# Attention scores on two row halves, and TensorE's order in periods of three pairs

## The chip, the cores and the metric

The kernel runs on one core of a Trainium2 chip. A core has TensorE (matmuls; PE in the profile, its weight loads PEld), VectorE (DVE), ScalarE (ACT), GpSimd (POOL) and SyncE (SP, which here issues the DMAs). Each engine works through its own queue in order and waits on semaphores for the others. TensorE writes to PSUM, eight banks of 128 partitions x 512 numbers of 32 bits. The metric is the time of one execution in microseconds (us), as the median of several runs; a profiled execution is recorded beside them.

## The reference

One layer of a hybrid backbone over 2048 latent tokens of width 1024 and 256 context tokens: a modulated norm, one input projection, two groups of heads, one output projection, and a SwiGLU FFN. The group that is changed is a softmax attention of 8 query heads on 2 key heads (4 query heads each), head width 64, over 2304 keys (context and latent):

```
def block(q):
    s = jnp.einsum('bqkgd,bnkd->bkgqn', q, keys).astype(jnp.float32) * scale
    p = jax.nn.softmax(s, axis=-1)
    return jnp.einsum('bkgqn,bnkd->bqkgd', p.astype(vals.dtype), vals)

o = lax.map(block, qb)
```

The other group is a gated linear recurrence in both directions over the same tokens (4 heads of width 128); its output and the attention's are concatenated ahead of the output projection.

## The kernel before, in words

An **item** is one query tile (128 queries) of one key head with its 4 query heads: 16 tiles x 2 key heads = 32 items. Keys come in 18 tiles of 128. Queries and keys are split in a high and a low part, since one pass of a matmul of the type used (fp32r) rounds its operands.

The softmax needs the maximum ahead of the exponentials, so an item passes over the scores twice.

*First pass* (`Item.chunk`, nine calls per item, one item ahead). A chunk takes 512 keys and two heads: two matmuls on 64 rows each (high part of the queries against high part of the keys), the one on rows 0 to 63, the other on rows 64 to 127 of the array, into two PSUM banks of one tile `mx` (line 930; the pool has one buffer). VectorE reduces the tile to `mn` (lines 936 and 940). The ninth chunk takes the last 256 keys for all four heads. `maxima` transposes the result (`pn`), copies it (`mr`) and writes it by four small DMAs into row 0 of `qb`.

*Second pass* (`Item.scores`, once for each key tile). Two matmuls on all 128 rows: `KS` (high and low key parts on the two halves) against `qa` (the high queries on both), line 962, and `KB` (a row of -1 and the high keys) against `qb` (the maximum and the low queries), line 963. ScalarE takes the Exp of the tile `s` (three banks) into half of a pair tile `p` (line 965). `KB` holds the high keys of one key head at a time and is loaded again where the second begins, and items 16 and 17 therefore compute their maximum on all 128 rows of `KS`. GpSimd adds two pair tiles of three (`ps`, line 972). `products` multiplies six key tiles with the values (line 981) and sums the weights by columns of ones (line 989) into one bank `av`; `finish` spreads the reciprocals (`pb`, line 1002) and scales the output.

*The order around it.* TensorE's order is the order of the program's text in this stage (a manual schedule); the other engines' order is set by the framework's scheduler. A tick is one key tile of one item. At each tick stand the scores, then steps of the recurrence (six of every nine ticks), then whatever `events` holds for the tick: chunks at ticks -3, -1, 0, 2, 3, 5, 7, 9 and 11 of the item before, loads and `maxima`. Every sixth tick has `products`, every ninth a round of the recurrence (`pa`, line 646), which reaches all engines. The recurrence shares two PSUM banks (`ps_h`) with `pn` and `pb`.

## Time and profile before

| what | value |
|---|---|
| median of 3 runs | 3408.22 us (3406.96 to 3409.92) |
| profiled execution | 3398.26 us |
| its span, first to last instruction | 3396.5 us |
| mean granted TensorE clock | 0.982 |
| attention stage, first scores to last | about 756 to 1842 us of the span |
| TensorE busy, whole span | 3235.6 us |
| first pass' reductions on VectorE (L936) | 256 of 1223 ns |
| Exp on ScalarE (L965) | 576 of 596 ns |

Rows of TensorE in the profile give the start, the duration, the line, the operation with what it writes and reads, the part of the array (rows*columns), the shape, and the count of instructions merged. Matmuls overlap with the next, so the distance of two starts is what one costs. `[0.18 <-DVE mn L936]` is idle time just before, and what ended it. A row of windows gives the stretch, the busy us of the five engine columns, the granted clock, the DMA share and GB/s. A row of groups gives busy us and the mean in ns after the first bar, idle us before it after the second.

### The profile page before, as it was taken

The numbers are of one execution on the slowest core, as the hardware profiler recorded it, in microseconds if no ns is written. First come the engines' busy times: TensorE is split into PE (matmuls) and PEld (weight loads), VectorE is DVE, ScalarE is ACT, GpSimd is POOL, SyncE is SP. The second block draws the span as 40 slices with busy tenths as digits, with TensorE's granted clock in tenths as the row PEclk, the third lists the DMA queues.
The fourth block names the chain that finished last, engine by engine and source line by source line (L and its number), as shares of the span: only waits on it lengthen the run. The fifth ranks groups of instructions, "written<-read, shape, count | busy, mean of one in ns | idle before, by whom it ended". The sixth has DMA issues, their size and how long they took to land. (4 is left out here: it accounts for less than half of the span.)

```text
span 3396.5 us, 55490 instructions
## 1 busy us (share of the span) xinstructions
PE 3235.6 (95%) x21212; PEld 2514.5 (74%) x21212; DVE 1725.5 (51%) x2742; ACT 1303.6 (38%) x2559; POOL 1636.5 (48%) x1450
## 2 busy tenths in 40 slices
PE   7999999979999999999999999999989989999998
PEld 5998977965666666656667887788868768888887
DVE  6344555224555455555553557444465743333566
ACT  4322222214444444444443224333344443333444
POOL 4322223105666666666644218776631357666222
PEclk9999999989999999999999999999989999999999
DMA  7243445341111111201105444444475543323754
GB/s 238 86 150 125 136 143 150 94 135 35 29 34 43 52 39 42 63 28 46 31 16 157 132 142 131 154 152 158 159 253 188 187 128 103 100 95 103 255 197 161
DMA packets 364459, 396.75 MB, mean 117 GB/s; under 512 B 30848, under 2 KB 261216, under 8 KB 363808
## 3 DMA queue, kind: packets, MB, share of 16 engines
q1 hardware_dynamic: 364192, 393.20, 36.2%
q8 instruction: 166, 2.72, 0.3%
q14 instruction: 101, 0.83, 0.1%
HBM read 271.90 MB, written 121.13 MB: 116 GB/s over the span
## 5 line engine op out<-in xcount | busy, mean ns | idle before, releaser
L936 DVE TENSOR_REDUCE mn<-mx 128x2 f32<-128x1024 f32 x256 | 313.2, 1223 | 418.8 <-PE mx L930 322.3
L965 ACT ACTIVATE p<-s 128x512 f32<-128x512 f32 x576 | 326.8, 596 | 469.8 <-PE s L963 467.9
L972 POOL TENSOR_TENSOR ps<-p,p 128x1024 f32<-128x1024 f32 x96 | 228.4, 2379 | 276.7 <-ACT p L965 276.5
L962 PE MATMUL s<-qa,K 128*128 128x512 f32 x576 | 271.3, 471 | 0.0
L981 PE MATMUL av<-p,VS 128*64 128x256 f32 x2304 | 270.6, 384 | 0.0
L963 PE MATMUL s<-qb,KB 128*128 128x512 f32 x576 | 232.5, 404 | 4.0 <-DMA KB<-s_k 3.2
L981 PEld LDWEIGHTS av<-p,VS 128*64 128x64 f32 x2304 | 158.1, 138 | 86.8 <-issue 15.7
L1500 POOL TENSOR_TENSOR y<-y,yg 128x512 f32<-128x512 f32 x48 | 76.1, 1600 | 284.1 <-DVE yg L1499 280.3
L930 PE MATMUL mx<-K,qa 64*128 64x512 f32 (+3 forms) x340 | 151.5, 470 | 63.3 <-DVE mn L936 63.2
L930 PEld LDWEIGHTS mx<-K,qa 64*128 64x128 f32 (+1 forms) x340 | 61.1, 190 | 163.9 <-DVE mn L936 127.7
L962 PEld LDWEIGHTS s<-qa,K 128*128 128x128 f32 x576 | 109.9, 191 | 71.1 <-issue 41.5
L1469 DVE TENSOR_TENSOR x<-lr,x 128x512 fp32r<-128x512 f32 x154 | 119.8, 813 | 67.2 <-ACT x L1468 64.5
L1469 DVE TENSOR_TENSOR dl<-lr,dh 128x512 fp32r<-128x512 f32 x154 | 118.6, 809 | 64.9 <-ACT dh L1468 64.8
L930 PE MATMUL mx<-KB,qa 64*128 64x512 f32 x300 | 138.9, 479 | 0.0
L1468 ACT ACTIVATE dh<-lr 128x512 fp32r<-128x512 f32 x154 | 89.4, 623 | 109.0 <-PE pd1A L1523 51.8
L343 PE MATMUL f<-hTh,wh 128*128 128x512 f32 (+1 forms) x320 | 122.4, 382 | 7.4 <-ACT ft L372 7.4
L1468 ACT ACTIVATE x<-lr 128x512 fp32r<-128x512 f32 x154 | 90.5, 626 | 93.8 <-PE pd0A L1523 38.5
L1330 PE MATMUL pA<-x,A11h 128*128 128x512 f32 x352 | 113.7, 403 | 9.7 <-ACT A11h L1303 7.4
L963 PEld LDWEIGHTS s<-qb,KB 128*128 128x128 f32 x576 | 111.2, 193 | 13.6 <-DMA KB<-s_k 3.5
L1523 PE MATMUL pd0A<-x,x 128*128 128x512 f32 x528 | 120.7, 389 | 0.0
L343 PE MATMUL f<-hTh,wl 128*128 128x512 f32 (+1 forms) x320 | 119.8, 375 | 0.0
L343 PE MATMUL f<-hTl,wh 128*128 128x512 f32 (+1 forms) x320 | 119.7, 374 | 0.0
(345 smaller groups left out, 9238.1 us busy)
## 6 DMA issues: line engine op xcount, KB each, us to landing
w<-in_w_gu_dram SPq DMA_DIRECT2D x88, 512.0 KB
wm<-in_w_mod_dram SPq DMA_DIRECT2D x24, 1024.0 KB
lr<-s_wT SPq DMA_DIRECT2D x88, 256.0 KB
lr<-in_w_down_dram SPq DMA_DIRECT2D x66, 256.0 KB
wq<-in_w_down_dram SPq DMA_DIRECT2D x44, 256.0 KB
s_wT<-wq SPq DMA_DIRECT2D x44, 256.0 KB
lr<-s_hid1S SPq DMA_DIRECT2D x44, 256.0 KB
lr<-s_hid0S SPq DMA_DIRECT2D x44, 256.0 KB
```

Source lines behind the costliest of these rows:

```text
L343: nc.tensor.matmul(pm[:, :n], w[wi][:, k, c0:c0 + P], hT[b][hi][:, k, :], start=(k == 0 and i == 0), stop=(k == KT - 1 and i == 2))
L930: nc.tensor.matmul(s[:, i, o:o + n], self.qa[ps, (h0 + i) * P:(h0 + i + 1) * P], K[ps, k0:k0 + n], start=True, stop=True)
L936: nc.vector.tensor_reduce(self.mn[:, h:h + 2, k], s, axis=AX.X, op=ALU.min)
L962: nc.tensor.matmul(s, KS[self.g][:, ks], self.qa, start=True, stop=False)
L963: nc.tensor.matmul(s, KB[:, ks], self.qb, start=False, stop=True)
L965: nc.scalar.activation(self.pairs[p][:, o:o + 512], s, AF.Exp, scale=-1.0)
L972: nc.gpsimd.tensor_tensor(t, self.pairs[p - 1], self.pairs[p], op=ALU.add)
L981: nc.tensor.matmul(self.av[i * 64:(i + 1) * 64, :256], VS[:, k, self.g * 64:(self.g + 1) * 64], self.pairs[k // 2][:, o:o + 256], start=(k ...
L1330: nc.tensor.matmul(acc, w[wi][:, k, :], x[xi][k], start=(start and k == 0 and i == 0), stop=(stop and k == KH - 1 and i == 2), skip_group_ ...
L1468: nc.scalar.activation(hi, src, AF.Copy)
L1469: nc.vector.tensor_tensor(lo, src, f32v(hi), op=ALU.subtract)
L1523: nc.tensor.matmul(cur[t], l[:, t * P:(t + 1) * P], r, start=(start and j == 0 and f == 0), stop=(stop and j == NHF - 1 and f == 2), skip_ ...
```

## The change

Second pass: a call of `scores` now makes a pair of key tiles, the even one on rows 0 to 63 and the odd one on rows 64 to 127. Four steps (high keys with high queries, low keys with high queries, high keys with low queries, and a row of -1 with the maximum) are each two matmuls on 64 rows, into two PSUM banks; the pool still has three. Keys are stored with the even tiles ahead of the odd ones; `KH` and `KL` hold the parts of both key heads for the whole stage, `KM` the row of -1, and `QM` the maximum, which is written once for each half (eight DMAs). Low queries are loaded on both halves.

First pass: a chunk is one head and 384 columns of both halves, so there are twelve per item, reduced in one go to one number.

Order: a period is three pairs and the products of these pairs; it has four chunks, one per quarter, and four steps of the recurrence. The first pair of the next period stands ahead of the products. The Exp's, sums and products themselves stay.

```
 def load_low(self):
-                self.qb = QB[self.n % 2]
-                nc.sync.dma_start(f32v(self.qb[64:, :]), s_q[self.g][self.qt, 1].rearrange("d h x -> d (h x)"))
+                self.qb = qpl.tile([P, 512], F32R, tag="qb", name=f"qb{self.nm}", bufs=2)
+                self.twice(self.qb, 1)
...
-                if c < 8:
-                    h, k = c // 4 * 2, c % 4
-                    part(0, h, k * 512, 512)
-                    nc.vector.tensor_reduce(self.mn[:, h:h + 2, k], s, axis=AX.X, op=ALU.min)
...
+                h, k = divmod(c, 3)
+                for i in range(2):
+                    rw = slice(i * 64, (i + 1) * 64)
+                    nc.tensor.matmul(s[:, i, :384], self.qa[rw, h * P:(h + 1) * P],
+                                     KH[self.g][rw, k * 384:(k + 1) * 384], start=True, stop=True)
+                nc.vector.tensor_reduce(self.mn[:, h, k:k + 1], s[:, :, :384], axis=AX.XY, op=ALU.min)
...
-                nc.tensor.matmul(s, KS[self.g][:, ks], self.qa, start=True, stop=False)
-                nc.tensor.matmul(s, KB[:, ks], self.qb, start=False, stop=True)
...
+                s = [ps_st.tile([P, 512], F32, tag="s", name=f"s{self.nm}_{p}{i}") for i in range(2)]
+                hi, lo = (K[self.g][:, p * P:(p + 1) * P] for K in (KH, KL))
+                ops = (hi, self.qa), (lo, self.qa), (hi, self.qb), (KM, self.qm)
+                for f, (k, q) in enumerate(ops):
+                    for i in range(2):
+                        rw = slice(i * 64, (i + 1) * 64)
+                        nc.tensor.matmul(s[i], k[rw, :], q[rw, :], start=(f == 0), stop=(f == 3))
+                for i in range(2):
+                    nc.scalar.activation(t[:, i * 512:(i + 1) * 512], s[i], AF.Exp, scale=-1.0)
...
-        CHUNKS = (-3, -1, 0, 2, 3, 5, 7, 9, 11)
...
+        chunks = {12 * (n - 1) - 5 + c: (it, c) for n, it in enumerate(items) if n for c in range(12)}
...
+                chunk(4 * x)
+                if b == 0 and n:
+                    items[n - 1].drain()
+                item.scores(GP * b + 1)
+                rest(0)
+                chunk(4 * x + 1)
+                rest(1)
+                item.scores(GP * b + 2)
+                if b == 0 and n:
+                    items[n - 1].finish(ps_h, "h")
+                chunk(4 * x + 2)
+                rest(2)
+                if x + 1 < NPER * NIT:
+                    items[(x + 1) // NPER].scores((x + 1) % NPER * GP)
+                made = rest(3)
+                if b == 1 and n + 1 < NIT:
+                    items[n + 1].maxima()
+                chunk(4 * x + 3)
+                next(made, 0)
+                item.products(b)
+                next(made, 0)
```

`rest(i)` makes one step of the recurrence, or a round of it at every sixth; `drain` copies the finished output and takes the reciprocals.

TensorE in item 12, just behind the products of item 11, before. A name `s12_0_3` is query tile 12, key head 0, key tile 3; `mx13_0_4` is chunk 4 of the next item.

```order
L962 MATMUL s12_0_3_12123<-qa12_0_11569,K0_7774 128x512
L963 MATMUL s12_0_3_12123<-qb0_7778,KB_7776 128x512
L930 MATMUL mx13_0_4_12129<-K0_7774,qa13_0_11945 128x512
L930 MATMUL mx13_0_4_12129<-KB_7776,qa13_0_11945 128x512
L962 MATMUL s12_0_4_12134<-qa12_0_11569,K0_7774 128x512
L963 MATMUL s12_0_4_12134<-qb0_7778,KB_7776 128x512
L962 MATMUL s12_0_5_12139<-qa12_0_11569,K0_7774 128x512
L963 MATMUL s12_0_5_12139<-qb0_7778,KB_7776 128x512
L930 MATMUL mx13_0_5_12143<-K0_7774,qa13_0_11945 128x512
L930 MATMUL mx13_0_5_12143<-KB_7776,qa13_0_11945 128x512
```

The same place now, where `s12_0_10` and `s12_0_11` are the two halves of pair 1:

```order
L930 MATMUL mx13_0_5_12772<-Kh0_7774,qa13_0_12329 128x384 x2
L957 MATMUL s12_0_10_12781<-qa12_0_11882,Kh0_7774 128x512
L957 MATMUL s12_0_11_12782<-qa12_0_11882,Kh0_7774 128x512
L957 MATMUL s12_0_10_12781<-qa12_0_11882,Kl0_7776 128x512
L957 MATMUL s12_0_11_12782<-qa12_0_11882,Kl0_7776 128x512
L957 MATMUL s12_0_10_12781<-qb12_0_12332,Kh0_7774 128x512
L957 MATMUL s12_0_11_12782<-qb12_0_12332,Kh0_7774 128x512
L957 MATMUL s12_0_10_12781<-qm0_7780,KM_7778 128x512
L957 MATMUL s12_0_11_12782<-qm0_7780,KM_7778 128x512
L930 MATMUL mx13_0_6_12799<-Kh0_7774,qa13_0_12329 128x384 x2
L957 MATMUL s12_0_20_12804<-qa12_0_11882,Kh0_7774 128x512
L957 MATMUL s12_0_21_12805<-qa12_0_11882,Kh0_7774 128x512
```

Chunks and scores are now alike in rows and columns of the array; between two pairs stands one chunk.

ScalarE at the same place before:

```order
L965 ACTIVATE p12_0_1_12082<-s12_0_2_12083 128x512
L965 ACTIVATE p12_0_1_12082<-s12_0_3_12123 128x512
L996 ACTIVATE ot11_0_12121<-av11_0_11856 128x256
L965 ACTIVATE p12_0_2_12133<-s12_0_4_12134 128x512
L965 ACTIVATE p12_0_2_12133<-s12_0_5_12139 128x512
```

And now, with the recurrence's M and C ahead of pair 1:

```order
L959 ACTIVATE p12_0_0_12682<-s12_0_00_12683 128x512
L959 ACTIVATE p12_0_0_12682<-s12_0_01_12684 128x512
L672 ACTIVATE M13_3_12913<-C13_2_12746 128x32x8
L619 ACTIVATE C14_0_12981<-F14_12795 128x512
L672 ACTIVATE M12_7_12924<-C12_6_12757 128x2x128
L673 ACTIVATE C13_4_13145<-C13_3_12914 128x16x2x8
L991 ACTIVATE ot11_0_12776<-av11_0_12459 128x256
L959 ACTIVATE p12_0_1_12780<-s12_0_10_12781 128x512
L959 ACTIVATE p12_0_1_12780<-s12_0_11_12782 128x512
```

The two Exp's of a pair follow each other, and work for the recurrence stands between pairs.

TensorE ahead of the first scores, before:

```order
L948 MATMUL pn0_0_7843<-identr_107,neg0_0_7841 4x128
L930 MATMUL mx1_0_0_7855<-K0_7774,qa1_0_7851 128x512
L930 MATMUL mx1_0_0_7855<-KB_7776,qa1_0_7851 128x512
L930 MATMUL mx1_0_1_7859<-K0_7774,qa1_0_7851 128x512
L930 MATMUL mx1_0_1_7859<-KB_7776,qa1_0_7851 128x512
L962 MATMUL s0_0_0_7868<-qa0_0_7794,K0_7774 128x512
```

And now:

```order
L941 MATMUL pn0_0_7866<-identr_107,neg0_0_7864 4x128
L930 MATMUL mx1_0_0_7879<-Kh0_7774,qa1_0_7808 128x384 x2
L930 MATMUL mx1_0_1_7883<-Kh0_7774,qa1_0_7808 128x384 x2
L930 MATMUL mx1_0_2_7887<-Kh0_7774,qa1_0_7808 128x384 x2
L930 MATMUL mx1_0_3_7891<-Kh0_7774,qa1_0_7808 128x384 x2
L930 MATMUL mx1_0_4_7895<-Kh0_7774,qa1_0_7808 128x384 x2
L957 MATMUL s0_0_00_7900<-qa0_0_7797,Kh0_7774 128x512
```

Five chunks of item 1 stand ahead of the first pair instead of two.

## The prediction

> **What bounds the kernel now.** I read the page first, then windows over the program's stages, then TensorE's own rows inside the stage that the change touches, then who waited for whom there.

> ```profile
> PE 3235.6 (95%) x21212; PEld 2514.5 (74%) x21212; DVE 1725.5 (51%) x2742; ACT 1303.6 (38%) x2559; POOL 1636.5 (48%) x1450
> 727.00:756.00 29.00, 8.44 (x29) 3.38 (x27) 16.41 (x20) 3.92 (x7) 5.62 (x5) 0.59 0.53 138
> 756.00:1842.00 1086.00, 1025.67 (x10009) 676.82 (x10010) 568.56 (x794) 494.42 (x1038) 667.89 (x711) 0.98 0.15 43
> ```

> TensorE is the bound of the whole program (95%) and of the attention stage, which lasts from 756 to 1842 us: 1026 of 1086 us there, while VectorE has 569, ScalarE 494 and GpSimd 668. Ahead of it lie 29 us of prelude in which TensorE works 8. All that changes lies in these 1115 us. A busy TensorE is not one at its peak, so I read starts, not durations:

> ```profile
> 1210.13 0.40 PE L963 MATMUL s<-qb,KB 128*128 128x512 f32 x1
> 1210.45 0.49 PE L930 MATMUL mx<-K,qa 64*128 64x512 f32 x1
> 1210.46 0.49 PE L930 MATMUL mx<-KB,qa 64*128 64x512 f32 x1
> 1210.88 0.50 PE L962 MATMUL s<-qa,K 128*128 128x512 f32 x1
> 1211.22 0.40 PE L963 MATMUL s<-qb,KB 128*128 128x512 f32 x1
> 1211.46 0.40 PE L962 MATMUL s<-qa,K 128*128 128x512 f32 x1
> 1211.69 0.40 PE L963 MATMUL s<-qb,KB 128*128 128x512 f32 x1
> 1212.28 0.39 PE L930 MATMUL mx<-K,qa 64*128 64x256 f32 x1 [0.18 <-DVE mn L936]
> 1212.28 0.50 PE L930 MATMUL mx<-KB,qa 64*128 64x256 f32 x2
> 1212.50 0.27 PE L930 MATMUL mx<-K,qa 64*128 64x256 f32 x1
> 1212.71 0.50 PE L962 MATMUL s<-qa,K 128*128 128x512 f32 x1
> ```

> Inside a run of scores, matmul follows matmul by 0.23 us (1211.46 to 1211.69). Around a maximum's chunk, which uses half the rows (64*128 beside 128*128), the steps are 0.32 (1210.13 to 1210.45), 0.42 and 0.34: 1.08 us instead of 3 x 0.23 = 0.69. So one chunk between scores costs 0.39 us for two changes of the array's setting, 0.20 each. The two halves of a chunk start 0.01 us apart, so they do run together.

> **Removed: changes of setting.** Counted along TensorE's order of this stage, 851 changes become 665: between full and half height 497 become 317, the others 354 become 348. 180 x 0.20 = **-36 us**. The scores' own work is the same: a pair of key tiles was 4 matmuls on full height and is now 8 on half height, two at a time: 4 steps of 0.23 both ways. The maximum streams the same 4608 columns per item and half (8 x 512 + 2 x 256 before, 12 x 384 after).

> **Removed: full-height chunks and one load.** Two items (16 and 17) computed their maximum on full height, one half after the other:

> ```profile
> L930 PE MATMUL mx<-K,qa 128*128 128x512 f32 x32 | 11.4, 439 | 4.0 <-DVE mn L936 4.0
> L930 PE MATMUL mx<-K,qa 128*128 128x256 f32 x8 | 1.4, 294 | 1.3 <-DVE mn L936 1.3
> ```

> They now take half the steps: 16 x 0.23 + 4 x 0.12, **-4 us**. The second head group's keys now have buffers of their own, so the single 3.2 us wait for KB goes (row below): **-3 us**.

> **Added: scores in pairs on three PSUM banks.** A pair takes two banks; with three in rotation, the second half's first matmul of the next pair needs the bank that the first Exp of this pair frees. TensorE goes in order, so everything behind stands still too.

> ```profile
> 1210.56 0.60 ACT L965 ACTIVATE p<-s 128x512 f32<-128x512 f32 x1 [2.96 <-PE s L963]
> 1211.66 1.09 ACT L965 ACTIVATE p<-s 128x512 f32<-128x512 f32 x2 [0.50 <-PE s L963]
> 1210.99 1.23 DVE L936 TENSOR_REDUCE mn<-mx 128x2 f32<-128x1024 f32 x1 [3.32 <-PE mx L930]
> 1212.27 0.18 PEld L930 LDWEIGHTS mx<-K,qa 64*128 64x128 f32 x1 [0.62 <-DVE mn L936]
> ```

> From the start of a pair's last matmul: 0.40 until it ends (1210.13 to 1210.53), 0.03 to the Exp, 0.60 for it, 0.05 back to TensorE (the reduction ends at 1212.22, the weight load that waits for it starts at 1212.27): 1.08 us, plus 0.11 for a weight load that waited and so isn't hidden. Without a wait the next pair would start 0.23 + 0.17 (a chunk of 384 columns) later. So 1.19 - 0.40 = 0.79 us are lost where only a chunk stands between two pairs. In the changed order 192 places have no products between two pairs; 74 of them hold nothing but a chunk (20 between pairs 1 and 2 of an item, 11 between 7 and 8, 1 between 4 and 5, 16 between 5 and 6, 26 between 8 and the next item's 0). The other 118 hold work of the recurrence or of the normaliser (L1002, the row is below) as well: 0.47 us for this one, or 0.2 in the smallest, with two changes of setting of 0.20 each, and that covers the wait. After a pair that itself began staggered (11 of the 26), the first half ends one step earlier: 0.55. 63 x 0.79 + 11 x 0.55 = **+56 us**. The ends: 0 if ScalarE were ahead, which its 0.60 excludes, and 192 x 0.79 = 152 if nothing covered. I keep 56, since the count is of places and the price of rows.

> ```profile
> 1202.41 0.71 PE L1002 MATMUL pb<-li,pick 128*128 128x128 f32 x4
> 1202.88 0.48 PE L962 MATMUL s<-qa,K 128*128 128x512 f32 x1
> ```

> **Moved: the maximum's chunks.** They were bunched, the waits for them are these:

> ```profile
> PE mx L930 <- DVE mn L936: 44.2, 95, 3.6
> PE s L963 <- DMA KB<-s_k: 3.2, 1, 3.2
> PE pn L948 <- DVE o L769: 3.1, 3, 1.2
> PE pn L948 <- DVE neg L943: 2.7, 1, 2.7
> PE pn L948 <- DVE Sb L739: 1.1, 1, 1.1
> ```

> Most of the 95 are of the 0.2 us kind seen at 1212.28; that part, some 14 us, lies inside the bare gaps from now on and is not paid twice: **-14**. The rest, 30 us, are a few long ones of this kind:

> ```profile
> 1020.23 0.95 DVE L994 RECIPROCAL li<-av 128x128 f32<-128x128 f32 x1
> 1021.09 0.11 DVE L683 TENSOR_REDUCE T<-T 128x8 f32<-128x16 f32 x1
> 1021.70 1.22 DVE L683 TENSOR_REDUCE T<-F 128x512 f32<-128x1024 f32 x1 [0.49 <-DMA F<-s_f]
> 1022.83 0.34 DVE L711 SCALAR_TENSOR_TENSOR S<-S,T,psf 128x128 f32<-128x128 f32 x1
> 1023.09 1.22 DVE L936 TENSOR_REDUCE mn<-mx 128x2 f32<-128x1024 f32 x1
> ```

> Here the recurrence's new unit stands ahead of the maximum in VectorE's queue and itself waits for its load. The changed order has the same operations in that queue, with 12 reductions per item instead of 9. I leave the 30 us where they are. The reductions shrink from 1024 to 768 elements (1.22 to about 0.92, an estimate by elements) and rise in number, 11.0 us per item both ways. New short waits: the last chunk of a period where neither a bare gap nor other work precedes it (12 places) and the transpose of the maximum (8 places), 0.4 each, 8 us, against the 7 us of pn that they replace: **+2** with rounding up.

> **Added: ScalarE's queue counts.** Before, a score tile could be two tiles ahead of ScalarE; now each pair leans on the Exp just before it, so an operation of the recurrence ahead of an Exp is felt at once.

> ```profile
> L672 ACT ACTIVATE C<-C 128x256 f32<-128x256 f32 x111 | 47.1, 424 | 20.6 <-POOL C L668 8.9 <-POOL kk L625 8.1
> L618 ACT ACTIVATE C<-F 128x512 f32<-128x512 f32 x15 | 10.2, 683 | 0.4
> ```

> One such 0.4 to 0.7 us in half of 32 items is **+8 us**; between 0 and the 30 us of a second set of long waits.

> **Prelude.** VectorE sets its pace, with TensorE's clock down (0.59 in the window):

> ```profile
> 749.05 1.23 DVE L936 TENSOR_REDUCE mn<-mx 128x2 f32<-128x1024 f32 x1 [0.89 <-PE mx L930]
> 751.17 1.23 DVE L940 TENSOR_REDUCE mn<-mx 128x4 f32<-128x1024 f32 x1 [0.89 <-PE mx L930]
> 753.83 1.23 DVE L936 TENSOR_REDUCE mn<-mx 128x2 f32<-128x1024 f32 x1 [1.22 <-PE mx L930]
> ```

> A chunk takes 2.12 us; one of 384 columns about 1.7. Twelve instead of nine: 20.4 against 19.1. Then five chunks of item 1 instead of two stand ahead of the first scores: 8.5 against 4.3, of which 1.6 is work that is missing later. **+5 us**, with bounds 0 and 8. Eight row copies of the maximum instead of four, and the low queries loaded twice, go through SyncE while five chunks or a whole period pass; with DMA at 0.15 of its time in the stage they cost nothing, and if that cover were gone, the one late copy per item would stop an item's first pair.

> **Sum.** -36 - 4 - 3 + 56 - 14 + 2 + 8 + 5 = **+14 us**. The profiled execution took 3398.3 us (span 3396.5), so 3412 for the like of it; the median of the runs shown lies 10 us higher, at 3408.2, so **3422 us**. A measurement of this kernel tells about 0.2% (7 us) from no change.

> One price has no row: the step of accumulating pairs on half height. The nearest is the second half-height step above: 1212.28 to 1212.50, 0.22 with 0.11 of unhidden load and 256 columns, so 0.11 for 256 and about 0.22 for 512 instead of 0.23; that would give up to 1152 x 0.01 = 11 us. I take 0.23 and keep the 11 for the range.

> **Rivals.**

> *Faster (0.31).* Spreading dissolves the long waits: a chunk now has a pair (0.93 us) or more before its bank is needed again, and the products (3.7 us) stand behind the fourth. If the 30 us go and the step is 0.22: 3422 - 30 - 11 = 3381; with half of that, about 3400. For it: 95 waits came from chunks one or two key tiles apart. Against: the long ones reach 3.6 us, more than a pair covers. It decides when more than 21 of the 30 us go.

> *No change (0.11).* A third of that, or bare gaps of 0.6 instead of 0.79: 74 x 0.19 = 14 us, 3408.

> *Much slower by queues (0.12).* Each of the 16 units' starts stops ScalarE or VectorE once more for 2 us, now also for the pairs: +32, 3454.

> *Weight loads come into the open (0.05).* If a half could not load its next weights while it streams, each of 1152 steps would grow by the 0.11 us that a visible load costs (0.34 against 0.23): 3422 + 127 = 3549. Against it:

> ```profile
> 1212.38 0.19 PEld L930 LDWEIGHTS mx<-K,qa 64*128 64x128 f32 x1
> 1212.39 0.19 PEld L930 LDWEIGHTS mx<-KB,qa 64*128 64x128 f32 x1
> ```

> Both halves' second weights load from 1212.38 while the first weights, loaded from 1212.28, stream on the same rows, and the next matmul starts at 1212.50. [...]

> **How the numbers follow.** Likeliest is the sum (0.41 with its own range 3408 to 3445). With the two slower rivals, slower by over 0.2% gets 0.58, no change 0.11, faster 0.31. The range from 3376 to 3470 leaves out the open weight loads and the tails.

> **What would show it.** Right: half-height scores 0.23 us apart, a new line of TensorE waiting for ScalarE's Exp of 50 us or more, waits for the maximum still above 30 us, the first scores about 5 us later. Wrong: waits for the maximum under 15 us (then faster), or steps of 0.34 between pairs' matmuls (then much slower).

## The result and the profile after

The changed kernel takes **3432.66 us** (median of 6 runs, 3424.65 to 3437.35), the kernel before beside it 3407.59 (6 runs, 3392.04 to 3411.95). The ratio is **1.0093 (95% interval 1.0071 to 1.0115)**: slower by 0.9%, some 32 us (24 to 39). The two medians as they stand lie 25 us apart. The forecast was 3422.

Profiled execution of the changed kernel, the page's first line and two windows, the prelude and the attention stage:

```profile
PE 3255.6 (95%) x22492; PEld 2551.3 (75%) x22492; DVE 1743.8 (51%) x2838; ACT 1298.3 (38%) x2559; POOL 1635.9 (48%) x1451
727.00:760.00 33.00, 11.81 (x52) 6.27 (x50) 16.26 (x23) 4.18 (x8) 5.65 (x5) 0.62 0.48 126
760.00:1870.00 1110.00, 1041.85 (x11279) 711.03 (x11280) 590.75 (x888) 490.79 (x1039) 673.72 (x712) 0.97 0.16 46
```

TensorE stays the bound, with 20 us more of busy time, and its clock in the stage is 0.97 where it was 0.98. The span grew by 27.5 us, from 3396.5 to 3424.0. Where, by the starts of single instructions:

| stretch | before | after | difference |
|---|---|---|---|
| span's start to first chunk of a maximum | 727.2 | 729.6 | +2.4 |
| prelude: first chunk to first scores | 28.6 | 35.3 | +6.7 |
| first scores to last products | 1091.2 | 1113.3 | +22.1 |
| last products to first matmul of the FFN (`pA`) | 189.0 | 184.6 | -4.4 |
| from there to the end | 1360.5 | 1361.2 | +0.7 |

Some 3 of the +22.1 us are work that only moved: 32 matmuls of the output projection now stand ahead of the last products where it was 19 (13 of 0.23 us), and the stretch behind is shorter for it.

The place where two pairs have only a chunk between them, TensorE's rows of the changed kernel and ScalarE's row beside it:

```profile
956.03 0.50 PE L957 MATMUL s<-qa,Kh 64*128 64x512 f32 x2
956.36 0.40 PE L957 MATMUL s<-qa,Kl 64*128 64x512 f32 x2
956.60 0.40 PE L957 MATMUL s<-qb,Kh 64*128 64x512 f32 x2
956.83 0.40 PE L957 MATMUL s<-qm,KM 64*128 64x512 f32 x2
957.07 0.33 PE L930 MATMUL mx<-Kh,qa 64*128 64x384 f32 x2
957.24 0.39 PE L957 MATMUL s<-qa,Kh 64*128 64x512 f32 x1
957.91 0.49 PE L957 MATMUL s<-qa,Kh 64*128 64x512 f32 x1 [0.28 <-ACT p L959]
957.91 0.72 PE L957 MATMUL s<-qa,Kl 64*128 64x512 f32 x2
958.25 0.62 PE L957 MATMUL s<-qb,Kh 64*128 64x512 f32 x2
958.49 0.62 PE L957 MATMUL s<-qm,KM 64*128 64x512 f32 x2
957.26 1.09 ACT L959 ACTIVATE p<-s 128x512 f32<-128x512 f32 x2 [0.53 <-PE s L957]
```

The first pair runs both halves together, 0.23 us from step to step (956.36, 956.60, 956.83). The chunk follows with no change of the array's setting, 0.24 after them. The first half of the next pair starts at 957.24 in the bank that was free; the second waits until the first Exp (957.26, two of 0.6 in the row) has emptied its bank, and starts at 957.91. From then on the halves are a step apart: the row at 958.49 covers 0.62 us with two matmuls of 0.39, so the last starts at 958.72. From a pair's last matmul (956.83) to the next pair's last it is 1.88, which is also the median over the 76 such places that the trace shows (11 of them take 1.65 to 1.76); without a wait it would be 1.10 (0.17 for the chunk, 0.93 for the pair).

Waits of TensorE between the first scores and the last products (matmuls), and of its weight loads; the last line is that of the kernel before:

```profile
PE mx L930 <- DVE mn L932: 31.8, 19, 4.9
PE s L957 <- ACT p L959: 9.1, 30, 0.5
PE mt L1136 <- DMA mix<-s_hg: 6.2, 3, 2.5
PEld mx L930 <- DVE mn L932: 81.7, 106, 5.3
PEld s L957 <- ACT p L959: 36.5, 85, 0.9
PEld s L962 <- ACT p L965: 11.8, 43, 0.4
```

The 95 waits for a maximum (44.2 us) became 19 (31.8 us, of which 1.05 still ahead of the first scores). Those under 1 us fell from 22 us to 4; those over 1 us were 12 with 22 us and are 12 with 27 us in the stage. The weight loads waited for the Exp before as well, 11.8 us, and do so for 36.5 now. New is a wait of 6.2 us for `mix`, the input of the output projection, near the stage's end. The longest wait for a maximum, on TensorE and then on VectorE, with the clock behind it:

```profile
854.91 0.39 PE L957 MATMUL s<-qm,KM 64*128 64x512 f32 x2
860.22 0.69 PE L930 MATMUL mx<-Kh,qa 64*128 64x384 f32 x2 [4.92 <-DVE mn L932]
858.08 1.22 DVE L684 TENSOR_REDUCE T<-F 128x512 f32<-128x1024 f32 x1 [4.77 <-DMA F<-s_f]
859.22 0.95 DVE L932 TENSOR_REDUCE mn<-mx 128x1 f32<-128x768 f32 x1
860.00:865.00 5.00, 4.78 (x46) 3.43 (x48) 3.55 (x7) 1.14 (x3) 4.99 (x8) 0.52 0.02 3
865.00:870.00 5.00, 4.87 (x63) 3.16 (x61) 2.11 (x3) 1.77 (x4) 3.13 (x6) 1.00 0.00 2
```

VectorE's queue has the recurrence's unit (`T<-F`) ahead of the maximum's reduction. `F` has one buffer, its load lands 4.77 us after VectorE could have begun, and TensorE, whose next chunk needs the tile `mx`, stands for 4.92 us. Then it runs at half clock (0.52) for the next window of 5 us, and at full clock after that.

### The profile page after: what moved, and what is told of

It is laid out like the page before. It is cut to its first block, busy times and chain, and to the rows that moved or that the text cites. A ratio compares the mean times of both kernels' runs of the same rounds, so it can differ in the third digit from the quotient of the medians.

```text
span 3424.0 us, 58458 instructions
## 1 busy us (share of the span) xinstructions
PE 3255.6 (95%) x22492; PEld 2551.3 (75%) x22492; DVE 1743.8 (51%) x2838; ACT 1298.3 (38%) x2559; POOL 1635.9 (48%) x1451
## 5 line engine op out<-in xcount | busy, mean ns | idle before, releaser
L932 DVE TENSOR_REDUCE mn<-mx 128x1 f32<-128x768 f32 x384 | 366.4, 954 | 441.1 <-PE mx L930 440.4
L959 ACT ACTIVATE p<-s 128x512 f32<-128x512 f32 x576 | 312.8, 594 | 442.4 <-PE s L957 437.0
L930 PE MATMUL mx<-Kh,qa 64*128 64x384 f32 x768 | 173.2, 431 | 62.9 <-DVE mn L932 53.7
L930 PEld LDWEIGHTS mx<-Kh,qa 64*128 64x128 f32 x768 | 77.8, 190 | 144.6 <-DVE mn L932 110.3
L957 PE MATMUL s<-qa,Kh 64*128 64x512 f32 x576 | 163.4, 453 | 9.7 <-ACT p L959 9.1
L957 PE MATMUL s<-qa,Kl 64*128 64x512 f32 x576 | 143.7, 415 | 0.0
L957 PE MATMUL s<-qm,KM 64*128 64x512 f32 x576 | 135.4, 398 | 1.4 <-DMA qm<-mr 0.9
L957 PE MATMUL s<-qb,Kh 64*128 64x512 f32 x576 | 135.1, 399 | 0.0
L1347 PE MATMUL pA<-x,S3h 128*128 128x512 f32 x352 | 112.0, 398 | 3.6 <-DVE x L1169 3.6
```

The source lines that it names most:

```text
L930: nc.tensor.matmul(s[:, i, :384], self.qa[rw, h * P:(h + 1) * P], KH[self.g][rw, k * 384:(k + 1) * 384], start=True, stop=True)
L932: nc.vector.tensor_reduce(self.mn[:, h, k:k + 1], s[:, :, :384], axis=AX.XY, op=ALU.min)
L957: nc.tensor.matmul(s[i], k[rw, :], q[rw, :], start=(f == 0), stop=(f == 3))
L959: nc.scalar.activation(t[:, i * 512:(i + 1) * 512], s[i], AF.Exp, scale=-1.0)
L1347: nc.tensor.matmul(acc, w[wi][:, k, :], x[xi][k], start=(start and k == 0 and i == 0), stop=(stop and k == KH - 1 and i == 2), skip_group_ ...
```

## The experiments

Each ratio is against the kernel before, run on the same chip; in microseconds it is taken of 3396, within 1.2 us of each median of the kernel before there. "F two buffers" below means that `F` gets a second buffer, and that the recurrence's states (`Sb`) shrink from eight buffers to six to make room.

### 1. Are changes of the array's setting worth 0.20 us each? (before, all chunks full height)

```diff
-                if self.n in (NCH, NCH + 1):
-                    sides = ((slice(0, P), KS[self.g]),) * 2
-                else:
-                    sides = ((slice(0, 64), KS[self.g]), (slice(64, P), KB))
+                sides = ((slice(0, P), KS[self.g]),) * 2
```

> The kernel before with all of the maximum's chunks on full height, as items 16 and 17 have them; nothing else is changed. Theory (a change between half and full height costs 0.20 us on TensorE, whatever the waits): the 465 such changes of the order before go, -93 us, and 30 items stream 2.2 us more each, +66 us: about 27 us faster than before, near 3381, no waits of TensorE added. Rival (the 0.39 us around a chunk are the wait for VectorE in another dress): the streaming is added and nothing is saved, 30 to 66 us slower.

3409.64 us, ratio 1.0046 (1.0032 to 1.0061): 16 us slower, which neither side had expected. The changes of setting, counted along the order as in the forecast, fell from 819 to 354. TensorE's rows in the stage, and its wait for the maximum there:

```profile
1198.88 0.39 PE L960 MATMUL s<-qb,KB 128*128 128x512 f32 x1
1199.11 0.63 PE L927 MATMUL mx<-K,qa 128*128 128x512 f32 x2
1199.58 0.40 PE L959 MATMUL s<-qa,K 128*128 128x512 f32 x1
1201.19 0.73 PE L927 MATMUL mx<-K,qa 128*128 128x512 f32 x2 [0.53 <-DVE mn L933]
PE mx L927 <- DVE mn L933: 63.9, 99, 3.8
```

The chunk no longer disturbs the scores' cadence (0.23, then twice 0.23), as intended. But the next chunk comes earlier to the one tile `mx` and waits for VectorE: the waits grew from 44.2 to 63.9 us. That is 20 of the 43 us between the forecast (27 faster) and the result; the rest was not located. Net of all waits, 465 changes less were worth 66 - 16 = 50 us here, 0.11 each, if the added streaming costs the 66 us that were estimated for it (4608 columns more in each of 30 items are 62 us, at the 0.23 us measured for 512): about half of the 0.20. This also brought a miscount to light: the order before has 819 changes and not 851, since items 16 and 17 have full-height chunks.

### 2. Is it the order or the form of the scores? (changed order, full-height scores and chunks)

Keys, low queries and the maximum are stored as in the kernel before; a key tile's scores are two matmuls, a pair's are four in a row.

```diff
-                for f, (k, q) in enumerate(ops):
-                    for i in range(2):
-                        rw = slice(i * 64, (i + 1) * 64)
-                        nc.tensor.matmul(s[i], k[rw, :], q[rw, :], start=(f == 0), stop=(f == 3))
...
+                    nc.tensor.matmul(s, KS[self.g][:, ks], self.qa, start=True, stop=False)
+                    nc.tensor.matmul(s, KB[self.g][:, ks], self.qb, start=False, stop=True)
```

> The changed order (periods of three pairs, twelve chunks of two times 384 keys, five chunks ahead of the first pair), with scores on full height again, tile by tile, and the chunks on full height. Theory (the loss comes from pairs that hold two of three score banks): TensorE's waits for the Exp go, about 60 us less than the changed kernel, and the setting changes between heights too; with the streaming added it comes out 15 to 35 us faster than before, 3375 to 3395. Rival (the order loses: spread chunks that meet VectorE's queue): it stays within 10 us of the changed kernel, about 3430, with waits for the maximum as large as there and hardly any for the Exp in either.

3391.94 us, ratio 0.9994 (0.9981 to 1.0006): level with the kernel before, short of the 15 to 35 us expected. So the order alone is not what costs; yet the gain expected of it did not come.

```profile
952.38 0.40 PE L953 MATMUL s<-qb,KB 128*128 128x512 f32 x1
952.90 0.30 PEld L930 LDWEIGHTS mx<-K,qa 128*128 128x128 f32 x2 [0.55 <-DVE mn L932]
952.90 0.62 PE L930 MATMUL mx<-K,qa 128*128 128x384 f32 x2
953.36 0.39 PE L952 MATMUL s<-qa,K 128*128 128x512 f32 x1
PE mx L930 <- DVE mn L932: 27.2, 19, 2.2
```

Hardly a wait for the Exp is left (1.2 us in the weight loads), but at such a place the chunk now comes 0.52 us after the scores where 0.23 would do: its weight load stood 0.55 us until VectorE had reduced the chunk before.

### 3. The same order, chunks on half height again

```diff
-                    rw, K = slice(0, P), KS[self.g]
+                    rw, K = (slice(0, P), KS[self.g]) if self.n in (NCH, NCH + 1) else \
+                        ((slice(0, 64), KS[self.g]), (slice(64, P), KB[self.g]))[i]
```

> The changed order with scores on full height tile by tile, as the run that came out level with before, but with the chunks on half height as in the kernel before. Against that run 492 changes of height come in (+98 us at 0.20 each) and 30 items stream 2.2 us less (-66 us). Theory (0.20 each): 20 to 40 us slower than it, 3410 to 3435. Rival (the changes fall into waits that are there anyway): level with it or up to 30 us faster.

3382.37 us, ratio 0.9953 (0.9935 to 0.9970): 14 us **faster** than experiment 2, although 492 changes of height came back. By the price of 0.20, less the 66 us of streaming that it saves, it should have been some 32 us slower. Net of all waits the 492 changes cost 66 - 14 = 52 us by that estimate, 0.11 each, the same as in experiment 1. Around a chunk the steps are 0.33, 0.38 and 0.33:

```profile
951.72 0.40 PE L954 MATMUL s<-qb,KB 128*128 128x512 f32 x1
952.05 0.44 PE L931 MATMUL mx<-K,qa 64*128 64x384 f32 x1
952.05 0.44 PE L931 MATMUL mx<-KB,qa 64*128 64x384 f32 x1
952.43 0.50 PE L953 MATMUL s<-qa,K 128*128 128x512 f32 x1
952.76 0.39 PE L954 MATMUL s<-qb,KB 128*128 128x512 f32 x1
PE s L954 <- issue: 5.2, 1, 5.2
```

That is 1.04 us in place of the 1.21 of experiment 2 (952.38 to 953.59). The two halves run together, so the chunk streams for half as long and the reduction of the one before it starts sooner: 0.49 us after a chunk's start in the changed kernel, whose chunks have this form too (904.86 to 905.35), where it is 0.66 in experiment 2 (951.23 to 951.89). Part of the changes falls into time in which VectorE would have been waited for.

This run splits the change. Against it, the changed kernel has the same order and differs in the scores' form and the operands for it: 1.0093 against 0.9953. (Two small things that the changed kernel does not have come with the old operands and make this run slower: one wait of 5.2 us, the last line, for which the profile names no releaser but which stands at the first scores against the newly loaded `KB`; and the full-height chunks of items 16 and 17, estimated at 4 us.) So **the pairs on half height cost about 48 us (34 to 61 by the two intervals), and the order, with its chunks of 384, gains about 16**; together the 32 that were measured.

### 4. One more bank for the pairs

One of the two banks that the recurrence shares was taken away and left empty (a):

```diff
-        ps_h = pool(hst, "ps_h", 2, PSUM)
+        ps_h = pool(hst, "ps_h", 1, PSUM)
```

or, beside that, given to the scores, so that each half of a pair has two banks (b):

```diff
-        ps_st = pool(st, "ps_st", 3, PSUM, side="right")
+        ps_st = pool(st, "ps_st", 2, PSUM, side="right")
...
+        ps_s1 = pool(hst, "ps_s1", 2, PSUM)
...
-                s = [ps_st.tile([P, 512], F32, tag="s", name=f"s{self.nm}_{p}{i}") for i in range(2)]
+                s = [(ps_st, ps_s1)[i].tile([P, 512], F32, tag="s", name=f"s{self.nm}_{p}{i}") for i in range(2)]
```

> The changed kernel with one bank instead of two for the recurrence, the maximum's transpose and the normaliser; the bank that comes free stays empty. It is the control for the next run. Both theories: slower than the changed kernel by 0 to 80 us, since each use of that bank waits for the last to be read.

> As the run before, with the free bank given to the scores: four banks, two for each half. Theory (the bare places lose 0.79 us each because the second half needs the bank of the first Exp): 50 to 60 us less than the control, and pairs follow each other in bare places after 1.1 us instead of 1.88. Rival (ScalarE's queue or VectorE sets these places anyway): within 10 us of the control, and the bare places stay near 1.88.

(a) 3545.06 us, ratio 1.0438 (1.0414 to 1.0463); (b) 3545.69 us, 1.0449 (1.0430 to 1.0468). The control alone is 117 us slower than the changed kernel, more than the 0 to 80 expected, and (b) is no faster where 50 to 60 us were forecast. So the total doesn't show the bank's price. The place itself does. TensorE in (b):

```profile
958.06 0.41 PE L958 MATMUL s<-qm,KM 64*128 64x512 f32 x2
958.29 0.35 PE L931 MATMUL mx<-Kh,qa 64*128 64x384 f32 x2
958.47 0.40 PE L958 MATMUL s<-qa,Kh 64*128 64x512 f32 x2
958.70 0.40 PE L958 MATMUL s<-qa,Kl 64*128 64x512 f32 x2
958.93 0.41 PE L958 MATMUL s<-qb,Kh 64*128 64x512 f32 x2
959.16 0.41 PE L958 MATMUL s<-qm,KM 64*128 64x512 f32 x2
```

From a pair's last matmul to the next pair's last it is 1.10 us, as worked out for no wait. So it is at 24 of the 76 places. Over all of them the median falls from 1.88 in (a) to 1.50 in (b), their sum from 155 to 117 us. So the wait for the third bank is there, and where nothing else is late it has the price given to it; but at 47 of the 76 places the chunk's weight load then waits for VectorE's reduction, so that the bank is worth 38 us in all. These 38 us came back elsewhere. Windows over the stage and the wait for the maximum, first (a), then (b):

```profile
765.00:1950.00 1185.00, 1044.29 (x11071) 707.27 (x11069) 578.89 (x875) 476.75 (x1013) 653.41 (x702) 0.96 0.14 39
PE mx L930 <- DVE mn L932: 24.6, 16, 4.4
```

```profile
765.00:1950.00 1185.00, 1030.89 (x11026) 704.59 (x11023) 579.68 (x872) 477.72 (x1013) 649.27 (x696) 0.94 0.13 37
PE mx L931 <- DVE mn L933: 32.5, 18, 5.2
```

The waits for the maximum took 8 us of it, and the clock fell from 0.96 to 0.94, some 24 us of 1185 (an estimate, to within 12 for the two decimals). Why it fell there, with one bank fewer for the recurrence in both, was not settled. What four banks for the pairs would be worth in the kernel itself therefore stays open.

### 5. The long waits: F two buffers, in the changed kernel and in the kernel before

```diff
-                self.F = up.tile([P, 512, 2], F32, tag="F", name=f"F{h}{u}", bufs=1)
+                self.F = up.tile([P, 512, 2], F32, tag="F", name=f"F{h}{u}", bufs=2)
```

> The changed kernel with two buffers instead of one for the tile F that each unit of the recurrence loads (and six instead of eight for the states Sb, for room). Theory (the long waits for the maximum are VectorE standing before a unit's first reduction, whose load can only start when the last unit has let F go; they also bring half-clock stretches of 3.4 us): the waits over 1 us mostly go, and the run is 25 to 45 us faster than the changed kernel, 10 us slower than before to 10 us faster. Rival (VectorE has too much to do at these places anyway): within 7 us of the changed kernel, the long waits stay under another name.

> The same two buffers in the kernel before. Theory: 15 to 30 us faster than before; so most of what the changed kernel pays for long waits the kernel before pays too, and it is no part of the difference. Rival (the kernel before has slack there, the changed one not): under 7 us, and then the long waits are part of the loss.

The changed kernel: 3404.66 us, ratio 1.0021 (1.0008 to 1.0034), so 24 us less than it took, just short of the 25 to 45 forecast. The kernel before: 3387.96 us, 0.9973 (0.9960 to 0.9986), 9 us less, between the theory's 15 and the rival's 7. TensorE's wait for the maximum in the stage, first the changed kernel, then the kernel before, each with two buffers:

```profile
PE mx L930 <- DVE mn L932: 15.4, 8, 2.9
```

```profile
PE mx L930 <- DVE mn L936: 41.3, 92, 2.0
```

In the changed kernel 16 of the 31.8 us went with the late load; in the kernel before 3 of 44.2. There 13 waits over 1 us are left, 19 us in all, behind other work in VectorE's queue. So about 15 us (24 less 9) of the difference between the kernels are the late load of `F`, which the changed order feels more. The waits for the Exp stayed (34.7 us in the weight loads), and so did the 1.88 us at the bare places.

### 6. Full-height chunks in two tiles of one bank each

What stood behind the changes of setting in experiments 1 and 2 was the one tile `mx` of two banks. Here it is two tiles of one bank, with a reduction for each.

```diff
-        ps_mx = pool(hst, "ps_mx", 1, PSUM)
+        ps_mx = pool(hst, "ps_mx", 2, PSUM)
...
-                s = ps_mx.tile([P, 2, 512], F32, tag="x", name=f"mx{self.nm}_{c}")
+                    s = ps_mx.tile([P, 512], F32, tag="x", name=f"mx{self.nm}_{c}{i}")
```

In the order before:

> The kernel before with chunks on full height, each head's half of a chunk in a tile of one bank with two buffers and a reduction of its own (18 of 512 elements per item instead of 9 of 1024). Theory (dropping the setting changes did free TensorE, but the freed time went into waits for the one chunk tile): the waits for the maximum fall from 64 us to under 30, and the run is 20 to 45 us faster than before. Rival (the changes of height are free): no faster than before.

3360.96 us, ratio 0.9888 (0.9868 to 0.9907): 38 us faster, as forecast, and 54 faster than experiment 1. The waits for the maximum:

```profile
PE mx L925 <- DVE mn L933: 19.4, 28, 2.5
```

In the changed order, with full-height scores:

> The changed order, scores on full height tile by tile, chunks on full height with each 384 keys in a one-bank tile of its own (two buffers, 24 reductions of 384 per item). Theory (with full-height scores the order itself costs nothing, and the waits of 0.28 us for the one chunk tile are what kept it level): 25 to 40 us faster than before, like the run in the old order. Rival (the order is worse by itself): 10 us or more slower than that run.

3347.63 us, ratio 0.9864 (0.9843 to 0.9885): 46 us faster than before, somewhat more than forecast, and 8 us ahead of the old order, less than the two intervals can tell apart.

### 7. Both, with F two buffers

> The old order with full-height chunks in one-bank tiles, and two buffers for the units' tile F. Theory (the two gains add, since one takes away short waits and the other long ones): 5 to 10 us faster than without the second buffer, 1.2 to 1.4% faster than before. Rival (two buffers of the maximum already ride over VectorE's long stops): no faster than without it.

> The changed order with full-height scores, one-bank chunk tiles and two buffers for F. Theory: 5 to 10 us faster than without the second buffer; with the long waits gone and chunks spread it is level with the same in the old order, within 10 us. Rival: the old order stays 10 us or more ahead.

Order before: 3347.36 us, ratio 0.9849 (0.9831 to 0.9867), 13 us from the second buffer. Changed order: **3325.13 us, ratio 0.9796 (0.9775 to 0.9818)**, the fastest, 2.0% ahead of the kernel before and 2.9% of the changed one. Here the second buffer gave 23 us where 5 to 10 were forecast, and the changed order is 18 us ahead of the old one where level within 10 was forecast; why it gains that much more was not traced. Its wait for the maximum and its stage:

```profile
PE mx L929 <- DVE mn L931: 8.6, 5, 2.1
752.00:1775.00 1023.00, 998.64 (x10180) 756.26 (x10182) 601.11 (x1236) 485.12 (x1026) 669.16 (x701) 0.99 0.16 46
```

TensorE waits for a maximum five times, and is busy 999 of 1023 us. The order with spread chunks is worth its gain here, once the scores are not in pairs.

## Why the prediction was right, and where it was off

The sign and the range held; the forecast was 11 us below the measured median. As a change it was too small, +14 us where 25 (by the medians) to 32 (by the ratio) came, and several terms were off in both directions. Its steps:

- **Scores' work unchanged (0.23 a step): right.** 956.36, 956.60, 956.83. The 11 us kept for a faster step did not come.
- **Weight loads come into the open: refuted.** The steps would be 0.34 and are 0.23. The next weights load while the matmuls before them stream on the same rows, step after step: the loads of 956.13, 956.37 and 956.60 (0.19 us each) under the matmuls of 956.03 (0.50), 956.36 and 956.60 (0.40 each).
- **Pairs on three banks, +56: right.** 76 places against 74 counted; 65 of them lose 0.78 us (0.79 in the forecast) and 11 lose 0.58 (0.55), in all some 57, if the few long waits for a maximum that fall there are left out. Experiment 4 shows that it is the bank: with a fourth one it is 1.10 us from pair to pair where VectorE is not late. At the other places VectorE stands behind the bank, so a fourth bank gave back 38 us there and not 57, and nothing in the total.
- **A new line of 50 us or more for the Exp: right in kind, too large as a number.** The trace books 36.5 us on the weight load that waits, 9.1 on the matmul; on the weight load 11.8 us of it were there before. A wait line doesn't hold the time that the staggered halves lose behind it; the distances do.
- **Removed changes of setting, -36: mis-sized.** Between full and half height 465 became 317 (in all 819 became 665), so 148 went and not 180: -30 at that price. And the price is not one that the whole kernel pays: net of all waits experiments 1 and 3 both give about 0.11 (by an estimate of the streaming), in part because changes lie in waits for VectorE; at that, -16. The 0.20 was read where nothing waited.
- **The maximum's chunks, -14 and 30 left: right in size by luck, as two errors cancel.** 44.2 us became 31.8. But the split was another: before, 22 us were short waits and 22 us long ones (over 1 us), not 14 and 30. The changed order did away with 18 us of the short ones, as it spreads the chunks, and the long ones did not stay but grew by 5. Nor is the unit's late load their whole cause: with two buffers for `F` the kernel before kept 41.3 us, where 19 us of long waits then stand behind other work of VectorE, while the changed kernel came down to 15.4. So the rival "faster" was right that spreading removes waits, but not that it removes the long ones, and the 21 of 30 us from which it was to decide were not reached.
- **ScalarE's queue, +8: not told apart.** No run tried it alone.
- **Prelude, +5: +6.7 measured.** The terms given for it come to 1.3 + 4.2 - 1.6 = 3.9, and the 1.6 would lie in the stage, so 5.5 is what compares. A chunk took 1.75 us (the reductions start at 750.63 and 752.38) where 1.7 was estimated, and TensorE stands for at least 1.05 us ahead of nearly all of them.
- **Not in the sum: the clock.** It was 0.98 in the stage and is 0.97. Behind many of TensorE's long waits, not all, stand 3.4 us or more at half clock (0.58 over the 4 us from 1168, 0.52 over the 5 us from 860). Added up over eleven windows of 100 us from 760 on, the shortfall is 18 us before and 29 after; the 11 us between them are an estimate to within a few us, since the clock is read to two decimals, and part of it may lie in waits. Some 4 us of the 29 lie around the waits for `mix` (0.53 over the 11 us from 1851).

With what was measured the stage gives -30 for the settings, -4 and -3 as forecast (not measured alone), +57 for the bare places, -12 for the waits for the maximum, +11 for the clock and +6 for `mix`: +25, where the table shows +22.1. With the settings at their net price, -16, it is +39. So the terms don't close to better than some 15 us, and that the forecast lay only 11 us off is partly luck: a term for the clock and one for `mix` were missing, and the settings were counted too high.

The pairs' 48 us of experiment 3 can be taken apart the same way: 57 for the bare places; less 176 changes of setting (841 against 665), 35 us at 0.20 or 19 at 0.11; 7 for the clock (in eleven windows of 100 us from the first scores on, the shortfall is 21 us in experiment 3 and 28 in the changed kernel); less 9 for `KB` and the full-height chunks; 4 for the waits for the maximum (27.7 there) and 5 for `mix` (1.4 there). That is 29 or 45, and the stage itself grew by 42, from 1071.5 to 1113.3 us. The bare places are the one large term in it.

## What to carry to other kernels

Before a saving on one engine is counted, look at what waits next: here a change of the array's setting cost 0.20 us where TensorE ran on, but only about 0.11 net over the whole kernel (experiments 1 and 3, an estimate), in part because VectorE's reduction of the one chunk tile was due there anyway. Chunks on full height, which drop the changes, lost 16 us; with that tile split in two as well (experiment 6) they gained 38. Work done in pairs needs its buffers in pairs: with three banks for tiles that come two at a time, most places without cover lost 0.78 us. A wait that shrinks in the profile after a reordering may only have been exchanged for another of the same size, so name its cause in each kernel by taking that cause away.

## What had not been expected of the hardware

```profile
1168.00:1172.00 4.00, 3.70 (x16) 3.09 (x18) 2.31 (x6) 0.00 (x0) 1.87 (x1) 0.58 0.00 0
1172.00:1176.00 4.00, 3.72 (x54) 2.64 (x54) 2.51 (x4) 2.78 (x6) 0.73 (x1) 0.99 0.41 131
1033.00:1036.00 3.00, 2.84 (x17) 1.70 (x17) 2.65 (x7) 2.92 (x9) 2.89 (x6) 1.00 0.66 176
```

  At half clock a step of the scores takes 0.42 us (1171.28 to 1171.70) where it is 0.23 a little later (1173.52 to 1173.75): such a wait costs its own length and about half of what follows, some 1.7 us (an estimate, half of the 3.4). Behind the longer wait of 2.79 us the clock stayed at 1.00, so the length alone doesn't decide; what does was not settled.
- Chunks on half height were faster than on full height where TensorE stands for VectorE's reduction of the chunk before (experiment 3 against 2: 14 us), although they bring two more changes of setting each: the two halves stream at the same time, and the reduction starts 0.49 us after the chunk's start (in the changed kernel, with chunks of the same form) where it was 0.66 in experiment 2.
